# Sixteen of the 44 gate/up groups of a two-layer decoder trunk computed by Strassen's scheme, and most transposes of their results sent through DRAM

## The chip, the cores and the metric

One core of one Trainium2 chip runs the whole program. The metric is the device time of one execution in microseconds (us), the median of several runs of the same program. Engines are named as in the profile: PE is TensorE's matmul, PEld its weight load, DVE is VectorE, ACT is ScalarE, POOL is GpSimd, and SP is SyncE, which here only issues the loads of the weights.

## What is computed

Two decoder layers over 256 tokens of width 2048 in float32: a gated DeltaNet mixer, an FFN, an HGRN2 mixer, an FFN, each behind an RMS norm and with a residual add, and a final norm. The change touches the two FFNs alone:

```
D_MODEL, SEQ, DEPTH = 2048, 256, 2
D_FF = -(-8 * D_MODEL // (3 * 256)) * 256        # 5632

def rmsnorm(x, w, eps=EPS):
    xf = x.astype(jnp.float32)
    y = xf * lax.rsqrt(jnp.mean(xf * xf, axis=-1, keepdims=True) + eps)
    return (y * w.astype(jnp.float32)).astype(x.dtype)

def swiglu(h, w_gate, w_up, w_down):
    return (jax.nn.silu(h @ w_gate) * (h @ w_up)) @ w_down
...
    for layer in range(DEPTH):
        ...
        h = h + swiglu(rmsnorm(h, ffn_norm[layer]), ffn_w_gate[layer], ffn_w_up[layer], ffn_w_down[layer])
    return rmsnorm(h, final_norm)
```

## The kernel before

**Float32 products out of three.** Each operand is split into a part that the matmul's fast 32-bit type holds and the rest: `wh` and `wl` for a weight, `xt_h` and `xt_l` for the activations. A product is xh*wh + xh*wl + xl*wh, three matmuls into one PSUM accumulator. ACT makes `wh` (a rounding copy of `raw`), DVE makes `wl` (`raw` - `wh`).

**The stream.** All weights come in items of 128 x 1024 values (512 KB), in one order, through `stream`: SP loads `raw`, ACT and DVE split it, PE uses it. There are four `raw` buffers (RAW_BUFS) and four each of `wh` and `wl` (SPLIT_BUFS), so a split can be made while the items ahead of it are still being used. Items of one result make a `Group`: its matmuls collect in one PSUM tile `main` (two of these, of two banks each), and its `end` reads them out. Four more banks, `aux`, serve everything else.

**The FFN.** The 5632 hidden columns are cut into 22 gate/up groups of 256 gate and 256 up columns. A group is eight items; each item holds two k-tiles of 128 rows and 512 columns (gate beside up), and each k-tile is used for two halves of 128 tokens, three matmuls each: 96 matmuls of 512 columns a group, with a piece of the activations as the stationary side. `gate_up`'s `end` takes Silu of the gate on ACT (`sg`), multiplies by up on DVE (`h1`), and, for every second group, turns the pair's `h1` (token x 512) into `turned` (512 x token) by 16 DVE transposes of 32 partitions x 256 (`turn`), and splits that into `hth` and `htl`, the stationary side of the down product. The norm's factor `rstd`, one number per token, is applied at the read-out. `down` multiplies by the down weights, in four column groups of 512, adds the residual (`add_x`, with x kept in DRAM as `x_home`), and calls what follows. FF_PARTS = (12, 10): twelve gate/up groups, their share of the down product, then ten and theirs.

**Who sets the order.** The program is first recorded, then a planner (`plan`) gives each engine its fixed order: matmuls of the stream (`main`, and `aux` tiles marked `stream`) stay in the order in which they are recorded, everything else is placed by a table of costs and by how late it may be, on PE between the stream's matmuls. Engines run that order without changing it, and wait for one another through semaphores. `Recorder.issue` emits it, so almost all instructions have its line, L490.

In the names of the profile and of the order, `h` is `h1`, `main<-wh,xt_h` a matmul into `main` with `wh` moving and `xt_h` stationary, and buffer numbers stand after a `_`.

Of the kernel before, what the change touches and what calls it, by code (L numbers as in the profile page):

```python
# [17 lines left out]
P = 128  # L18
T = 256
# [5 lines left out]
FF_PARTS = (12, 10)  # L25
N_HGRN = 4
LEVELS = (64, 32, 16, 8, 4, 2, 1)
MASKED = LEVELS[2:]
AHEAD = 3
# [465 lines left out]
class Group:  # L495

    def __init__(self, chunks, mm, end, begin=None, apart=False, cols=False):
        self.chunks, self.mm, self.end, self.begin, self.apart = chunks, mm, end, begin, apart  # L500
        self.cols = cols
        self.halves = [
            c[:, at : at + 1024] for c in chunks for at in range(0, c.shape[1], 1024)
        ]


class Trunk:
# [22 lines left out]
    def apart(self):  # L530
        return self.aux(stream=True), self.aux(stream=True)

# [55 lines left out]
    def stream(self, groups):  # L588
        nc = self.nc
        flat = [(g, i) for g in groups for i in range(len(g.halves))]  # L590
        ready = {}

        def place(tag, g):
            w = self.tile(self.wsplit, [P, 1024], tag, F32R, ordered=True)
            v = nc.virtual(w)
            v.pad, v.cols = PAD, g.cols
            return w

        def load(n):
            g, i = flat[n]  # L600
            raw = self.tile(self.wraw, [P, 1024], "raw", ordered=True)
            nc.sync.dma_start(raw, g.halves[i])
# [3 lines left out]
            h = place("wh", g)  # L606
            nc.scalar.activation(h, raw, AF.Copy)
            low = place("wl", g)
            nc.vector.tensor_tensor(out=low, in0=raw, in1=h.bitcast(F32), op=ALU.subtract)
# [3 lines left out]
        for n, (g, i) in enumerate(flat):  # L613
            while loaded < min(n + AHEAD, len(flat)):
                load(loaded)
                loaded += 1
            if i == 0:
                if g.begin:
                    g.begin()
                g.ps = self.apart() if g.apart else self.main()  # L620
            g.mm(g.ps, i, *ready.pop(n))
            if i == len(g.halves) - 1:
                g.end(g.ps)
# [143 lines left out]
    def turn(self, out, x):  # L767

        out = out.rearrange("p n (t a s) -> p t n a s", t=2, s=32)
        x = x.rearrange("p t (n b s) -> p t n b s", n=4, s=32)  # L770
# [5 lines left out]

    def ffn(self, j, after):
        nc, a = self.nc, self.a
        hts, h1s = {}, {}

        def gate_up(gi):
            def end(ps):
                if gi % 2 == 0:
                    h1s[gi // 2] = self.tile(self.pool, [P, 2, 512], "h1", bufs=2)
                h1 = h1s[gi // 2]
# [976 lines left out]
```

## Time and profile before

| what | value |
|---|---|
| time, median of 3 runs (lowest to highest) | 2762.76 us (2762.22 to 2763.23) |
| the profiled execution: its time, its span | 2763.82 us, 2761.4 us |
| granted TensorE clock, mean | 0.999 |
| loads of gate/up weights, first and last issue | 806.2 us, 2623.3 us |
| loads of HGRN2 weights, first and last issue | 1529.8 us, 1913.0 us |
| turns of `h1` on DVE | 352 transposes, 153.5 us busy, 436 ns each |
| DVE's splits `wl` | 945, 1160.6 us busy, 1229 ns each |
| bytes moved | 580.52 MB, 210 GB/s |

The span is the time from the first to the last instruction of the profiled execution; its time lies 2.4 us above it. The first FFN lies between the last GDN products and the first HGRN2 load, the second runs from about 2036 us to the end. Busy time of an engine counts overlapping instructions once; on PE the ends of matmuls are modelled, so that the rate of a run of matmuls is read from their starts.

### The profile page before, as it was taken

To read this page: it belongs to the slowest core of one execution; us is meant where nothing else is said; L and a number is where in the kernel's file an instruction comes from. 1 tells how busy PE (TensorE), PEld (TensorE's weight loads), DVE (VectorE), ACT (ScalarE), POOL (GpSimd) and SP (SyncE) were. 2 spreads that over 40 slices of the span, in tenths; PEclk is the share of its full clock that TensorE was granted. 3 is DMA by queue.
4 is the path that set the end of the run, shared out by engine and by line. 5 is a ranking of instruction groups with operands and counts; after the bars stand their busy time and mean duration, and the time that the engine had idled before them with its cause. 6 is when DMAs were issued, how large, how long until landed. Compare 5 with 4: busy or idle time off the path is not lost.

```text
span 2761.4 us, 41091 instructions
## 1 busy us (share of the span) xinstructions
PE 2744.9 (99%) x15662; PEld 2328.7 (84%) x15662; DVE 1899.6 (69%) x2857; ACT 1428.3 (52%) x2010; POOL 251.4 (9%) x370
## 2 busy tenths in 40 slices
PE   9999999999999999999999999999999999999998
PEld 9888888888888888888888989988888888888887
DVE  7787888887766667546665687778657675456764
ACT  6646666565554444344444556556454444344443
POOL 1213222232110000000000100000100000000000
PEclk9999999999999999999999999999999999999999
DMA  7686668787786666766667655555776666766664
GB/s 260 201 281 222 190 211 284 210 276 219 225 256 203 195 193 193 225 224 194 193 192 219 221 166 179 172 166 178 236 257 192 193 194 209 224 209 193 193 201 160
DMA packets 162677, 580.52 MB, mean 210 GB/s; under 512 B 20138, under 2 KB 21306, under 8 KB 162352
## 3 DMA queue, kind: packets, MB, share of 16 engines
q1 hardware_dynamic: 138912, 503.15, 57.1%
q0 software_dynamic: 23280, 73.91, 8.5%
q8 instruction: 122, 2.00, 0.3%
q10 hardware_dynamic: 288, 0.85, 0.1%
q14 instruction: 75, 0.61, 0.1%
HBM read 550.52 MB, written 27.31 MB: 209 GB/s over the span
## 4 chain that ended last, share of the span: by engine, by line
PE 98%; ACT 0%; DVE 0%; issue 0%; DMA 0%; SPq 0%; POOLq 0%; POOL 0%; ACTq 0%
PE main L490 92%; PE aux L490 6%; DMA first<-in_x 0%; ACT dec L490 0%; DVE wl L490 0%; ACT wh L490 0%; DVE utmp L490 0%; SPq L490 0%; DVE pre L490 0%; ACT xt_h L490 0%; DVE u L490 0%; ACT y L490 0%; POOLq L1758 0%; ACT junk L490 0%; DVE xl L490 0%
## 5 line engine op out<-in xcount | busy, mean ns | idle before, releaser
L490 DVE TENSOR_TENSOR wl<-raw,wh 128x1024 fp32r<-128x1024 f32 x945 | 1160.6, 1229 | 754.3 <-ACT wh L490 742.6
L490 ACT ACTIVATE wh<-raw 128x1024 fp32r<-128x1024 f32 x945 | 1000.9, 1060 | 1221.8 <-PE main L490 1123.5
L490 PE MATMUL main<-wh,xt_h 128*128 128x512 f32 x2176 | 849.3, 390 | 0.8 <-ACT wh L490 0.8
L490 PE MATMUL main<-wl,xt_h 128*128 128x512 f32 x2176 | 848.5, 390 | 1.3 <-DVE wl L490 1.3
L490 PE MATMUL main<-wh,xt_l 128*128 128x512 f32 x2176 | 849.5, 390 | 0.0
L490 PEld LDWEIGHTS main<-wl,xt_h 128*128 128x128 f32 x2176 | 408.5, 188 | 85.6 <-DVE wl L490 1.6
L490 PEld LDWEIGHTS main<-wh,xt_h 128*128 128x128 f32 x2176 | 408.5, 188 | 85.1 <-ACT wh L490 1.2
L490 PEld LDWEIGHTS main<-wh,xt_l 128*128 128x128 f32 x2176 | 408.6, 188 | 84.5
L490 PE MATMUL main<-xt_h,wh 128*128 128x256 f32 (+1 forms) x1040 | 288.8, 278 | 0.7 <-ACT wh L490 0.7
L490 PE MATMUL main<-xt_h,wl 128*128 128x256 f32 (+1 forms) x1040 | 288.3, 277 | 0.9 <-DVE wl L490 0.9
L490 PE MATMUL main<-xt_l,wh 128*128 128x256 f32 (+1 forms) x1040 | 288.1, 277 | 0.3 <-DVE xt_l L490 0.3
L490 PE MATMUL main<-wh,htl 128*128 128x512 f32 x664 | 258.6, 389 | 0.0
L490 PE MATMUL main<-wl,hth 128*128 128x512 f32 x664 | 258.4, 389 | 0.0
L490 PE MATMUL main<-wh,hth 128*128 128x512 f32 x664 | 258.3, 389 | 0.0
L490 PEld LDWEIGHTS main<-xt_h,wh 128*128 128x128 f32 (+1 forms) x1040 | 194.5, 187 | 1.3 <-ACT wh L490 0.9
L490 PEld LDWEIGHTS main<-xt_h,wl 128*128 128x128 f32 (+1 forms) x1040 | 194.4, 187 | 1.2 <-DVE wl L490 1.1
L490 PEld LDWEIGHTS main<-xt_l,wh 128*128 128x128 f32 (+1 forms) x1040 | 194.4, 187 | 1.0 <-DVE xt_l L490 0.5
L490 DVE STREAM_TRANSPOSE turned<-h 32x256 f32<-32x256 f32 x352 | 153.5, 436 | 7.2
L490 PE MATMUL main<-wh,ot_l 128*128 128x512 f32 x384 | 151.3, 394 | 0.0
L490 PE MATMUL main<-wl,ot_h 128*128 128x512 f32 x384 | 150.5, 392 | 0.0
L490 PE MATMUL main<-wh,ot_h 128*128 128x512 f32 x384 | 150.5, 392 | 0.0
L490 PEld LDWEIGHTS main<-wl,hth 128*128 128x128 f32 x664 | 124.6, 188 | 25.9
(206 smaller groups left out, 2249.9 us busy)
## 6 DMA issues: line engine op xcount, KB each, us to landing
raw<-in_ffn_gu SPq DMA_DIRECT2D x352, 512.0 KB, 4.7
raw<-in_ffn_d SPq DMA_DIRECT2D x176, 512.0 KB, 4.8
raw<-in_hgrn_in SPq DMA_DIRECT2D x128, 512.0 KB, 4.0
raw<-in_gdn_kq SPq DMA_DIRECT2D x64, 512.0 KB, 5.6
raw<-in_gdn_v SPq DMA_DIRECT2D x64, 512.0 KB, 4.7
raw<-in_gdn_z SPq DMA_DIRECT2D x64, 512.0 KB, 4.8
raw<-in_gdn_out SPq DMA_DIRECT2D x64, 512.0 KB, 5.0
x_home<-x POOLq DMA_DIRECT2D x36, 512.0 KB, 6.3
```

Source lines behind the costliest of these rows:

```text
L490: getattr(getattr(tc.nc, op.eng), op.method)(*args, **kw)
```

## The change

**Mixed groups.** In eight of the 22 groups of each FFN (pairs 1, 4, 7 and 8) the 2x2 block product [A11 A12; A21 A22] x [B11 B12; B21 B22] is computed with seven block products. The blocks of A are the two halves of the tokens and the two halves of the 2048 rows; the blocks of B are those rows by gate and by up (256 columns). With s1 = A21 - A22, s2 = A11 - s1, s3 = A21 - A11, s4 = A12 - s2 and t1 = B11 + B12, t2 = B22 + B12, t3 = B22 + t1, t4 = t3 + B21, the products are P1 = A11 B11, P2 = A12 B21, P3 = s4 B22, P4 = A22 t4, P5 = s1 t1, P6 = s2 t3, P7 = s3 t2. Each is a half bank of 128 tokens x 256 columns, in four `aux` banks, over 8 k-tiles and three matmuls: 168 matmuls of 256 columns.

`mix_inputs` makes s1 to s4 once an FFN on DVE, from `xt_h` + `xt_l` times `rstd_row`, and splits them into `mixh` and `mixl` (for this, `rstd_row` is now made at each layer's start). For each of four steps `kk` of a mixed group two halves of the weights are loaded into a ring of four tiles `sraw`; DVE makes t1 to t4 in the other two, and all are split as before (of the first half only B11). The group's `end` combines the seven products, with `rstd` only on P1, P2 and P4.

**Order.** FF_PARTS becomes (8, 8, 6), and FF_PLAN writes out which mixed pair lies among which plain pairs or among the down items of the part before. `Group` gives way to single `Item`s, which `among` interleaves.

**Turns.** All pairs but 3, 6 and 10 (FF_QUICK) are turned through DRAM: four DVE transposes of 128 x 256 into `blocks`, one DMA to `blocks_home`, and four DMAs back into `turned`, on POOL's queue. The quick pairs are turned on DVE as before, but a group at a time, in 32 transposes of half the size.

```diff
-FF_PARTS = (12, 10)
+FF_PARTS = (8, 8, 6)
+FF_PLAN = (
+    "0 | 1:2,3",
+    "4:down | 7:5,6",
+    "8:down | 9 | 10",
+)
+FF_QUICK = (3, 6, 10)
...
+def among(few, many, tail):
+    out, done = [], 0
+    for i, item in enumerate(many):
+        out.append(item)
+        upto = min(len(few), -(-len(few) * (i + 1) // (len(many) - tail)))
+        out += few[done:upto]
+        done = upto
+    return out
...
-            raw = self.tile(self.wraw, [P, 1024], "raw", ordered=True)
-            nc.sync.dma_start(raw, g.halves[i])
+            raw = item.ring() if item.ring else self.tile(self.wraw, [P, 1024], "raw", ordered=True)
+            if item.src is not None:
+                nc.sync.dma_start(raw, item.src)
...
+            if item.pre:
+                item.pre(raw)
...
+    def turn_through(self, out, x):
...
+        for b in range(4):
+            self.nc.vector.transpose(
+                blocks[:, b, :].rearrange("p (n t s) -> p n t s", n=4, s=32), x[:, :, :, b, :]
+            )
+        self.nc.gpsimd.dma_start(home, blocks)
+        home = home.rearrange("(a f) b r -> b f a r", a=4)
+        for b in range(4):
+            self.nc.gpsimd.dma_start(out[32 * b : 32 * b + 32], home[b])
...
+            uses = {
+                1: (plain(0, 0), 0, 0), 2: (plain(2, 0), 0, 1), 3: (mixed(4), 1, 0), 7: (mixed(3), 1, 1),
+                5: (mixed(1), 2, 0), 6: (mixed(2), 2, 1), 4: (plain(2, 1), 3, 0),
+            }
...
+            def raw_ring():
+                return self.tile(self.pool, [P, 1024], "sraw", bufs=4, ordered=True)
...
+                def mm(wh, wl):
+                    for k in range(2):
+                        for n, cols in parts:
+                            sh, sl = uses[n][0](2 * kk + k)
+                            c = slice(cols(k), cols(k) + T)
+                            for m, (x, w) in enumerate(((sh, wh), (sh, wl), (sl, wh))):
+                                nc.tensor.matmul(
+                                    product(n), x, w[:, c],
...
+                items += [
+                    item(kk, halves[0], keep(0), [(1, lambda k: k * 512)], lambda x: quarters(x)[:, 0]),
+                    item(kk, halves[1], keep(1), [(2, lambda k: k * 512), (3, lambda k: k * 512 + T)]),
+                    item(kk, None, sums(0), [(5, lambda k: k * T), (7, lambda k: 512 + k * T)]),
+                    item(kk, None, sums(1), [(6, lambda k: k * T), (4, lambda k: 512 + k * T)]),
+                ]
...
+        items = self.gdn(self.next_input(1, True))
+        items += self.ffn(0, self.next_input(2, True))
+        items += self.hgrn(self.next_input(3, True))
```

**What moves, in three places.** PE in the first FFN, where the first mixed item begins. Before, the same stretch holds nothing but products of 512 columns:

```order
L490 MATMUL main_8903<-wh_8844,xt_l_16_72 128x512
L490 MATMUL main_8903<-wh_8864,xt_h_13_69 128x512
L490 MATMUL main_8903<-wl_8874,xt_h_13_69 128x512
L490 MATMUL main_8903<-wh_8864,xt_l_17_73 128x512
L490 MATMUL main_8903<-wh_8864,xt_h_13_69 128x512
```

and now, behind the last matmuls of a plain item (`wh_9210`), the products P1, P2 and P3 of the first step:

```order
L496 MATMUL main_9276<-wl_9246,xt_h_12_68 128x512
L496 MATMUL main_9276<-wh_9210,xt_l_16_72 128x512
L496 MATMUL aux_9300<-wh_9237,xt_h_12_68 128x256
L496 MATMUL aux_9300<-wl_9265,xt_h_12_68 128x256
L496 MATMUL aux_9300<-wh_9237,xt_l_16_72 128x256
```

One token half and 256 columns stand where two halves and 512 stood, and the accumulators are `aux` tiles.

DVE at the end of the first plain group. Before, it made one `wl` after another:

```order
L490 TENSOR_TENSOR wl_9089<-raw_9026,wh_9078 128x1024
L490 SCALAR_TENSOR_TENSOR h_1337_8885<-main_8903,rstd_59,sg_8886 128x256
L490 SCALAR_TENSOR_TENSOR h_1337_8885<-main_8903,rstd_59,sg_8887 128x256
L490 TENSOR_TENSOR wl_9110<-raw_9044,wh_9099 128x1024
L490 TENSOR_TENSOR wl_9128<-raw_9062,wh_9118 128x1024
```

and now:

```order
L496 TENSOR_TENSOR wl_9265<-sraw_8895,wh_9237 128x2x256
L496 TENSOR_TENSOR wl_9270<-sraw_8899,wh_9253 128x1024
L496 TENSOR_TENSOR sraw_9282<-sraw_8899,sraw_8900 128x512
L496 TENSOR_TENSOR mixl_8888<-h_1325_9234,mixh_8887 128x512
L496 TENSOR_TENSOR wl_9295<-raw_9177,wh_9278 128x1024
L496 TENSOR_TENSOR sraw_9282<-sraw_9282,sraw_8899 128x512
L496 SCALAR_TENSOR_TENSOR h_1348_9256<-main_9106,rstd_59,sg_9288 128x256
L496 TENSOR_TENSOR wl_9324<-sraw_8900,wh_9303 128x1024
L496 TENSOR_TENSOR wl_9337<-raw_9195,wh_9319 128x1024
L496 TENSOR_TENSOR wl_9345<-sraw_9282,wh_9334 128x1024
L496 TENSOR_TENSOR sraw_9359<-sraw_8901 128x512
```

Between two plain splits (`raw`) stand the sums into `sraw`, the splits of the mixed items and the last of `mix_inputs`; `sraw_8899` is read for the last time in the sixth of these rows, and its place is the next step's second half.

DVE at the turn of a pair. Before, the 16 transposes lay in runs of two to four between splits:

```order
L490 STREAM_TRANSPOSE turned_8888<-h_1337_8885 32x2x4x32 x3
L490 TENSOR_TENSOR wl_9283<-raw_9211,wh_9271 128x1024
L490 STREAM_TRANSPOSE turned_8888<-h_1337_8885 32x2x4x32 x4
L490 TENSOR_TENSOR wl_9307<-raw_9230,wh_9292 128x1024
L490 STREAM_TRANSPOSE turned_8888<-h_1337_8885 32x2x4x32 x3
```

and now, for the second half of pair 3:

```order
L496 TENSOR_TENSOR htl_8910<-turned_10490,hth_8909 128x512
L496 SCALAR_TENSOR_TENSOR h_1571_10301<-main_10290,rstd_59,sg_10536 128x256
L496 TENSOR_TENSOR sraw_10728<-sraw_10650 128x512
L496 TENSOR_TENSOR wl_10736<-raw_10597,wh_10716 128x1024
L496 TENSOR_TENSOR wl_10743<-sraw_10641,wh_10732 128x1024
L496 STREAM_TRANSPOSE turned_10490<-h_1571_10301 32x2x2x32 x16
L496 TENSOR_TENSOR wl_10807<-raw_10633,wh_10753 128x1024
```

The 16 transposes of that half now stand in one block ahead of the next `wl`.

More of the change, by code (lines that the diff above doesn't have):

```diff
@@ L813, in down @@
+        def down(part, cg, pairs):
             w = a[f"ffn_d{j}_{part}"]
+            lo = sum(FF_PARTS[:part]) // 2
             def operand(kt):
-                h, l = hts[first + kt // 4]
+                h, l = hts[pairs[kt // 4]]
                 return h[:, kt % 4, :], l[:, kt % 4, :]
```

331 lines of the change are left out of this document (244 added, 87 removed).

## The prediction

> **What bounds the kernel now.** I read the profile's first page, then the chain that ended last, then what TensorE waited for, then windows and timelines inside the feed-forward layers (FFN).
>
> ```profile
> PE 2744.9 (99%) x15662; PEld 2328.7 (84%) x15662; DVE 1899.6 (69%) x2857; ACT 1428.3 (52%) x2010; POOL 251.4 (9%) x370
> PE 98%; ACT 0%; DVE 0%; issue 0%; DMA 0%; SPq 0%; POOLq 0%; POOL 0%; ACTq 0%
> 828.78 636.50 PE main L490 x2808
> 2036.53 687.72 PE main L490 x3034
> PE main L490 <- DVE wl L490: 2.2, 2, 1.3
> ```
>
> The first row is busy time by engine, the second the chain by engine, the next two are the longest pieces of that chain (start, length), the last is PE's longest wait for another engine (total, times, longest). TensorE is busy from end to end; each FFN is one unbroken run of matmuls, and PE waited twice for a `wl` in the whole program. So the time falls by what is taken from PE, as long as VectorE (DVE) and ScalarE (ACT) keep the operands coming. In a plain FFN stretch they have room:
>
> ```profile
> 880.00:920.00 40.00, 40.00 (x179) 33.11 (x178) 25.88 (x33) 18.32 (x20) 0.00 (x0) 1.00 0.59 191
> 2639.97 1.06 ACT L490 ACTIVATE wh<-raw 128x1024 fp32r<-128x1024 f32 x1 [1.66 <-PE main L490]
> 2641.06 1.23 DVE L490 TENSOR_TENSOR wl<-raw,wh 128x1024 fp32r<-128x1024 f32 x1 [1.50 <-ACT wh L490]
> ```
>
> The window row has start:end, length, then busy time of PE, PEld, DVE, ACT, POOL, the granted clock (1.00) and the DMA share. ACT waits for PE to give back a `wh` buffer (four exist), DVE waits for ACT: both run as far ahead as the buffers let them.
>
> **PE's part: what 1/8 fewer columns are worth.** Two timelines of PE alone, first and last row of an even run:
>
> ```profile
> 1419.78 0.39 PE L490 MATMUL main<-wh,xt_h 128*128 128x512 f32 x1
> ...
> 1423.86 0.39 PE L490 MATMUL main<-wh,xt_h 128*128 128x512 f32 x1
> ```
> ```profile
> 39.79 0.28 PE L490 MATMUL main<-xt_h,wh 128*128 128x256 f32 x1
> ...
> 43.87 0.28 PE L490 MATMUL main<-xt_h,wh 128*128 128x256 f32 x1
> ```
> ```profile
> L490 PEld LDWEIGHTS main<-wh,xt_h 128*128 128x128 f32 x2176 | 408.5, 188 | 85.1 <-ACT wh L490 1.2
> L490 PEld LDWEIGHTS main<-xt_h,wh 128*128 128x128 f32 x1024 | 192.3, 188 | 1.3 <-ACT wh L490 0.9
> L490 PE MATMUL aux<-vjunk,ones x8: 270/274/275, 33.6 to 1557.4; 128*128 128x128 f32 x8
> ```
>
> In the first, 18 matmuls of 512 columns start in 4.08 us, 226.7 ns each; in the second 36 of 256 columns start in 4.08 us, 113.3 ns each, with one 128-column weight load per matmul in both (the first two rows of the third block: count, busy time, mean ns). Half the columns cost exactly half. A plain group has 16 k-tiles x 2 token halves x 3 = 96 matmuls of 512: 21.76 us. A mixed group has 7 products x 8 k-tiles x 3 = 168 of 256: 19.04 us. Saved: 2.72 us a group, 16 groups, **43.5 us**. In the measured 256-column case the weight was the stationary side and x moved; now x is stationary. Both load in the same 188 ns, and the 113 ns hid that load, so I take 113.3.
>
> The Trainium skill ("TensorE: Matmul & The Clock Gate", section "Wait — 56ns, not 53.3ns?") gives each matmul a fixed extra of about 2.5 ns. By that the 1152 additional matmuls would give back 2.9 us, an estimate from that page; the two runs above show no fixed part, so the trace speaks against it and it is not in the sum.
>
> PE also gets two rows of `rstd_row` more (two matmuls each, like the last row's 0.27 us): +1.2 us, rounded up.
>
> **DVE's part: does it still keep up?** This decides. DVE's busy time counts overlapping instructions; what matters in a full queue is start to start.
>
> ```profile
> 1704.43 0.69 DVE L490 TENSOR_TENSOR kp<-k,e 128x512 f32<-128x512 f32 x1
> 1705.04 0.68 DVE L490 TENSOR_TENSOR qp<-q,e 128x512 f32<-128x512 f32 x1
> 1705.64 1.22 DVE L490 TENSOR_TENSOR wl<-raw,wh 128x1024 fp32r<-128x1024 f32 x1
> 1706.78 1.28 DVE L490 TENSOR_TENSOR e<-b 128x512 f32<-128x512 f32 x2
> ...
> 1684.08 0.42 DVE L490 TENSOR_TENSOR e<-b 128x256 f32<-128x256 f32 x1
> 1684.42 0.29 DVE L490 COPY e<-b 128x256 f32<-128x256 f32 x1
> ...
> 2037.47 1.65 DVE L490 SCALAR_TENSOR_TENSOR xt_l<-aux,head,xt_h 128x256 fp32r<-128x256 f32 x4
> ...
> 2656.17 2.25 DVE L490 STREAM_TRANSPOSE turned<-h 32x256 f32<-32x256 f32 x5
> ```
>
> Steps: 0.60 us for 512 elements, 1.14 for 1024, 0.34 for 256, 0.39 for scalar_tensor_tensor of 256 ((1.65 - 0.48)/3), 0.45 for a transpose of 256. The quick turn's half-size transposes (128 elements) are not in the trace: between half and all of 0.45, I take 0.33.
>
> A mixed step (`kk`) splits one 512 and three 1024 tiles and adds four 512: 0.60 + 3 x 1.14 + 4 x 0.60 = 6.4 us; a mixed pair of groups has eight, 51.4, plus two ends of 0.39 + 6 x 0.34 + 0.60 = 3.0: 57.5 us. A turn through DRAM costs DVE 4 x 0.45 + 1.14 = 2.9 us (16 x 0.45 + 1.14 = 8.3 before); a quick pair 32 x 0.33 + 2 x 0.60 = 11.8. `mix_inputs` is 8 x 1.14 + 16 x 0.60 = 18.7 an FFN. By stretch of FF_PLAN, DVE against PE:
>
> - pairs 0, 1, 2, 3: 18.7 + six plain groups (48 x 1.14 + 12 x 0.39 = 59.4) + 57.5 + three turns 8.8 + 11.8 = 156 us; PE 6 x 21.76 + 2 x 19.04 = 169 us. 93%.
> - pairs 7, 5, 6: 39.6 + 57.5 + 5.9 + 11.8 = 115; PE 125. 92%.
> - each mixed pair beside a down part: 32 x 1.14 + 4 residual adds of 1.14 + 57.5 + 2.9 = 102; PE 125. 81%. The four residual adds that the third part brings to each FFN are in here.
>
> With the full durations in place of the steps (1.23, 0.68, 0.42) the first two come to 170 and 124, just PE's own time. Can DVE run that full? HGRN's windows answer:
>
> ```profile
> 1680.00:1720.00 40.00, 40.00 (x305) 34.82 (x305) 36.02 (x45) 26.65 (x32) 1.04 (x1) 1.00 0.59 184
> 1690.00:1700.00 10.00, 10.00 (x49) 8.41 (x49) 9.69 (x10) 6.14 (x8) 1.04 (x1) 1.00 0.58 186
> 1700.00:1710.00 10.00, 10.00 (x72) 8.13 (x71) 9.34 (x14) 6.60 (x8) 0.00 (x0) 1.00 0.61 184
> ```
>
> DVE 90% busy over 40 us and 95% over 20 us, PE never idle. So on average DVE keeps up. What remains is local. From the two rows at 2640, a `wl` is done 2.3 us after its `wh` could start, while three items are still ahead on PE: 3 x 2.72 - 2.3 = 5.9 us of lead between plain items, but 2.72 + 2 x 1.36 - 2.3 = 3.1 us with two mixed items (12 matmuls of 113 ns) among the three. The second halves of quick pairs 3 and 6 put 16 transposes in one block before the next `wl`: 5.3 us, 2.2 more than the lead. Four such places: **+8.8 us** (0 if the lead is whole there, up to 16 x 0.45 - 3.1 = 4.1 each). Pair 10's second half must be evacuated, turned and split within the four down items ahead of it (10.9 us) while DVE makes their `wl`: 5.3 + about 2 + 4 x 1.14 = 11.9: **+1 us**, twice.
>
> **ACT, DMA, POOL.** ACT splits the same tiles: 4 x (0.63 + 3 x 1.06), two copies and two Silus of 256, 17 us a mixed group, inside PE's 19 and the plain groups' slack (18.32 of 40 busy above). Bytes loaded stay; 16 turns of 512 KB add 8 MB each way.
>
> ```profile
> L490 ACT ACTIVATE wh<-raw 128x1024 fp32r<-128x1024 f32 x945 | 1000.9, 1060 | 1221.8 <-PE main L490 1123.5 <-ACT sg L490 16.8 <-ACT hth L490 15.2
> L490 ACT ACTIVATE junk<-x 128x512 f32<-128x512 f32 x34 | 21.5, 632 | 3.9 <-DVE x L490 3.4
> L490 ACT ACTIVATE sg<-main,rstd 128x256 f32<-128x256 f32 x88 | 36.3, 461 | 0.0
> raw<-in_ffn_gu SPq DMA_DIRECT2D x352, 512.0 KB, 4.7
> x_home<-x POOLq DMA_DIRECT2D x36, 512.0 KB, 6.3
> x<-x_home POOLq DMA_DIRECT2D x36, 512.0 KB, 5.7
> L490 DVE TENSOR_TENSOR wl<-raw,wh x44: 1218/1226/1226, 1120.6 to 1237.5; 128x1024 fp32r<-128x1024 f32 x44
> L490 DVE TENSOR_TENSOR wl<-raw,wh x105: 1199/1226/1943, 1639.0 to 1959.2; 128x1024 fp32r<-128x1024 f32 x105
> ```
>
> A `sraw` tile of step kk+1 can load only when DVE's sums of step kk have read the tile; behind that wait on SP stand the plain `raw` loads. By the new order about 6.5 us of DVE work lie between that release and the first use, a load lands in 4.7: hidden, with 1.8 to spare. A turn takes 3 (end) + 1.8 + 6.3 + 5.7 + POOL's issues of about 3 + split 2, some 22 us; pair 1's is wanted after six plain items and four down items with theirs between, about 32 us. POOL's queue holds the residual stores and loads behind it, wanted later still. All at nothing; if that cover went, a late pair would stop PE by the difference.
>
> The last two rows are DVE's `wl` (shortest/median/longest) while POOL only issued DMAs, and in HGRN, where POOL also copies and fills. The Trainium skill ("GPSIMD Engine Reference", Specifications) has POOL share its SBUF interface with DVE instructions of two SBUF inputs, which all added sums are. The second row fits (one of 1943 ns), but the first shows that issuing DMAs, all that POOL gains here, stretches nothing.
>
> **Sum.** Profiled execution 2763.8 (span 2761.4 and 2.4 around it) - 43.5 + 1.2 + 8.8 + 2 = 2732.3. That execution lies 1.1 above the median of the runs (2762.8), so **2731**.
>
> **Rivals.**
> - *All hidden*: the lead covers the blocks; 2763.8 - 42.3 - 1.1 = 2720. For it: the 20 us at 95% above. Against: shorter items, less lead.
> - *DVE paces the heavy stretches*: dependent sums don't overlap, so full durations count, at the 95% that HGRN showed: (170 + 124)/0.95 = 309 against PE's 294, 15.4 an FFN, 2751. For it: 93% leaves 23 us an FFN. Against: most neighbours in the new order are independent.
> - *DVE stands behind late inputs* (the other side): its queue is in order, and each wait for a `sraw` load, a product or ACT's `wh` holds all splits behind it. At full durations it decides from 294/(294 + 21) = 93% busy; at the 87% of a GDN slice (row below) it would be 338 against 294, +88, 2808: slower. Against: the HGRN rows.
> ```profile
> 320.00:360.00 40.00, 40.00 (x252) 32.73 (x252) 34.63 (x72) 21.84 (x34) 13.57 (x21) 1.00 0.79 241
> ```
> - *Turns land late*: 8 us at three places of each FFN, +48: 2768, about no change. Against: the 10 us of room.
> - *256 columns do not cost half* with x as the stationary side: from 129.5 ns a matmul (21.76/168) nothing is saved; with the load's own 188 ns unhidden it would be 31.6 us a group, 2921. Against: GDN's even 113.3.
>
> **How the numbers follow.** Chances: the forecast 0.45 (its own range 2724 to 2742), all hidden 0.25, DVE pacing 0.13, late inputs 0.08, late turns 0.06, dear matmuls 0.03. About 0.2% (5.5 us) can be told from no change. Faster: the first three and a third of the late turns, 0.85; same 0.04; slower 0.11. The range 2719 to 2754 takes the first three and leaves out 0.17.
>
> **What would show it.** PE: 128x256 matmuls `aux<-wh,...` at even 113 ns starts. PE's waits on DVE `wl` some 10 us in all, sitting at pairs 3 and 6; DVE some 90% busy from the start of each FFN for about 170 us. None on `htl` from a turn through DRAM, none on DMA. Wrong if PE's idle time exceeds 40 us, or if it is spread evenly over all mixed items (then DVE paces them), or if DVE's waits name `sraw` loads.

## The result: half of the forecast gain

| | before | changed |
|---|---|---|
| median of four runs each, us | 2762.99 | 2746.83 |
| range, us | 2762.22 to 2765.33 | 2745.67 to 2747.26 |
| changed / before | | 0.9939 (95%: 0.9922 to 0.9957) |
| profiled execution, us (span) | 2763.82 (2761.4) | 2747.26 (2745.6) |

The kernel became 16.2 us faster, where 31.8 were forecast. The time lies in the range, between the forecast and no change. From the page of the changed kernel, busy time by engine and the chain that ended last by engine:

```profile
PE 2727.6 (99%) x16822; PEld 2363.9 (86%) x16822; DVE 2169.4 (79%) x3309; ACT 1548.5 (56%) x2192; POOL 308.4 (11%) x466
PE 98%; ACT 0%; DVE 0%; issue 0%; DMA 0%; SPq 0%; POOLq 0%; POOL 0%; ACTq 0%
```

PE sets the end as before. It was idle for 2745.6 - 2727.6 = 18.0 us, before for 2761.4 - 2744.9 = 16.5. So idle time rose by 1.5 us, where 10.8 were forecast, and PE's busy time fell by 17.3 us, where 42.3 were forecast: no engine held PE up, and its own work became dearer than forecast. That is more than the whole of the 15.6 us that were expected and not seen. What PE waited for, the three longest sums and the row of the quick turns (total, times, longest):

```profile
PE main L496 <- DVE wl L496: 2.2, 2, 1.3
PE aux L496 <- DMA first<-in_x: 1.7, 2, 1.4
PE main L496 <- ACT wh L496: 1.5, 2, 0.8
...
PE main L496 <- ACT hth L496: 1.0, 4, 0.2
```

The first is the same row as before the change. There is no wait on a `wl` by a mixed item at all, none on a turn through DRAM and none on a `sraw` load; the quick turns show up as the last row, four waits on `hth` of 0.24 us. Two windows of the first FFN, the second around the quick turn of pair 3, in the columns of the prediction:

```profile
880.00:920.00 40.00, 40.00 (x231) 35.30 (x230) 34.63 (x44) 22.86 (x27) 2.79 (x5) 1.00 0.69 225
1000.00:1040.00 40.00, 39.74 (x226) 34.57 (x226) 37.74 (x56) 22.03 (x24) 2.90 (x5) 1.00 0.64 203
```

DVE is busy 34.63 and 37.74 of 40 us (25.88 in the first before), 87 and 94%, and PE keeps its 40.00 and 39.74. Now PE's own timeline in the changed kernel, one mixed item and what follows it (start, us):

```profile
903.07 0.28 PE L496 MATMUL aux<-wh,xt_h 128*128 128x256 f32 x1
903.18 0.28 PE L496 MATMUL aux<-wl,xt_h 128*128 128x256 f32 x1
903.30 0.28 PE L496 MATMUL aux<-wh,xt_l 128*128 128x256 f32 x1
...
904.38 0.28 PE L496 MATMUL aux<-wh,mixl 128*128 128x256 f32 x1
904.50 0.40 PE L496 MATMUL main<-wh,xt_h 128*128 128x512 f32 x1
904.73 0.40 PE L496 MATMUL main<-wl,xt_h 128*128 128x512 f32 x1
904.97 0.39 PE L496 MATMUL main<-wh,xt_l 128*128 128x512 f32 x1
...
905.66 0.39 PE L496 MATMUL main<-wh,xt_l 128*128 128x512 f32 x1
```

From 903.30 to 904.38 nine matmuls of 256 columns start in 1.08 us: 120.0 ns each, not 113.3. And after 904.50 five of 512 columns take 1.16 us, 232 ns each, before they return to 226.7. Over all 224 places where a mixed item is followed by plain ones, the five take 233, 236, 228, 233 and 231 ns (medians), together 27 ns above five times 226.7, while the first two of a mixed item take 7 ns less together than 2 x 120.

The starts of the whole trace, as means from one start to the next (gaps over 300 ns left out), in ns:

| | mixed, 256 columns | x stationary, 512 (gate/up and mixers) | down, 512 | projections with x moving, 256 |
|---|---|---|---|---|
| before | none | 226.90 | 226.71 | 114.65 |
| changed | 119.41 | 227.55 | 228.31 | 114.85 |

From these the account: 1,536 matmuls of 226.90 go (-348.5 us), 2,688 of 119.41 come (+321.0), a net -27.5 in place of -43.5. The 4,992 matmuls of 512 columns with x stationary that stay (2,688 of gate/up, the others in the two mixers, whose price did not move) are 0.65 ns dearer (+3.2), the 2,112 of the down projection 1.60 (+3.4). With 1.5 us more of idle time and 1.2 for the `rstd_row`s this is -18.2; the profiled executions differ by 16.6, which leaves 1.6 us. One window, in the changed kernel and before, shows a candidate (the column ahead of the last two is the granted clock):

```profile
8.00:12.00 4.00, 3.76 (x19) 3.76 (x20) 3.79 (x8) 3.22 (x9) 0.00 (x0) 0.57 0.98 355
```
```profile
8.00:12.00 4.00, 3.22 (x28) 3.22 (x29) 3.93 (x8) 3.63 (x11) 0.00 (x0) 1.00 0.98 355
```

Behind a wait of 1.42 us for the first inputs, the changed kernel's profiled execution has 3.4 us at a granted clock of 0.50, which is worth some 1.7 us.

So two questions go to the experiments: why does a matmul of 256 columns cost 120.0 ns here and 113.3 ns in the projections, and what do the changes of width cost? A third is whether DVE's headroom and the turns through DRAM were needed at all.

One thing differs between the two kinds of 256-column matmul beside the roles of x and the weight. The kernel pads its weight tiles so that in the groups with `cols` the stationary `wh` and `wl` lie at bytes 108 and 364 modulo 512 of a partition (`IN_COLS`); everything else that a large matmul reads, stationary or moving, plain or mixed, lies at byte 32 by the kernel's layout. That makes two theories: **placement** (the price hangs on where the operands lie) and **role** (a matmul with x stationary costs 6.7 ns more anywhere).

### The profile page after: what moved, and what is told of

Its sections match the earlier page's. It is cut to its first block, busy times and chain, and to the rows that moved or that the text cites. A ratio compares the mean times of both kernels' runs of the same rounds, so it can differ in the third digit from the quotient of the medians.

```text
span 2745.6 us, 44285 instructions
## 1 busy us (share of the span) xinstructions
PE 2727.6 (99%) x16822; PEld 2363.9 (86%) x16822; DVE 2169.4 (79%) x3309; ACT 1548.5 (56%) x2192; POOL 308.4 (11%) x466
## 4 chain that ended last, share of the span: by engine, by line
PE 98%; ACT 0%; DVE 0%; issue 0%; DMA 0%; SPq 0%; POOLq 0%; POOL 0%; ACTq 0%
PE main L496 81%; PE aux L496 18%; DMA first<-in_x 0%; ACT dec L496 0%; DVE wl L496 0%; ACT wh L496 0%; DVE utmp L496 0%; SPq L496 0%; DVE pre L496 0%; ACT xt_h L496 0%; DVE u L496 0%; ACT mixh L496 0%; POOLq L2007 0%; ACT junk L496 0%; DVE p L496 0%
## 5 line engine op out<-in xcount | busy, mean ns | idle before, releaser
L496 ACT ACTIVATE wh<-raw 128x1024 fp32r<-128x1024 f32 x817 | 864.4, 1059 | 937.9 <-PE main L496 803.2
L496 DVE TENSOR_TENSOR wl<-raw,wh 128x1024 fp32r<-128x1024 f32 x817 | 1003.1, 1229 | 426.4 <-ACT wh L496 416.8
L496 PE MATMUL main<-wh,xt_h 128*128 128x512 f32 x1664 | 651.8, 392 | 0.8 <-ACT wh L496 0.8
L496 PE MATMUL main<-wl,xt_h 128*128 128x512 f32 x1664 | 651.0, 391 | 1.3 <-DVE wl L496 1.3
L496 PE MATMUL main<-wh,xt_l 128*128 128x512 f32 x1664 | 650.6, 391 | 0.0
L496 PEld LDWEIGHTS main<-wh,xt_l 128*128 128x128 f32 x1664 | 312.6, 188 | 65.2
L496 PEld LDWEIGHTS main<-wh,xt_h 128*128 128x128 f32 x1664 | 312.9, 188 | 62.8 <-ACT wh L496 1.2
L496 ACT ACTIVATE wh<-sraw 128x1024 fp32r<-128x1024 f32 (+1 forms) x256 | 243.4, 951 | 141.6 <-PE main L496 98.1
L496 DVE TENSOR_TENSOR wl<-sraw,wh 128x1024 fp32r<-128x1024 f32 (+1 forms) x256 | 278.4, 1088 | 28.2 <-ACT wh L496 26.8
L496 PEld LDWEIGHTS main<-wh,htl 128*128 128x128 f32 x680 | 127.7, 188 | 29.1 <-DVE htl L496 1.7
```

The source lines that it names most:

```text
L496: getattr(getattr(tc.nc, op.eng), op.method)(*args, **kw)
```

## Experiments

Times are medians, and the ratio is to the kernel before on the same chip, with its 95% interval. Prices are means from start to start, as in the table above.

**The projections' weights at byte 32.**

```diff
-            v.pad, v.cols = PAD, cols
+            v.pad, v.cols = PAD, False
```

> The changed kernel with one thing altered: the projections that run the other way round (weight tile stationary, x moving, 256 columns) keep their weights in SBUF at the byte offset that the rows groups use (32 modulo 512) instead of 108 and 364. In the changed kernel these 3,072 matmuls start every 113.3 ns, while the 2,688 of the mixed groups (x stationary, 256 columns too) start every 120.0 ns. Theory 'placement' (the price of a matmul beside its columns hangs on where its two operands lie in SBUF): the 113.3 ns become 120.0, 3,072 x 6.7 ns = 20.5 us more, about 2,767 us. Theory 'role' (a matmul with x stationary and the weight moving costs 6.7 ns more wherever its operands lie): they stay at 113.3 ns and the time stays near 2,747 us.

Measured: 2766.02 us, ratio 1.0008 (0.9998 to 1.0017); against the changed kernel's ratio that is 0.69% or 19 us more. An even run of the projections in the changed kernel, and the same in this one:

```profile
39.10 0.28 PE L496 MATMUL main<-xt_h,wh 128*128 128x256 f32 x1
...
44.54 0.28 PE L496 MATMUL main<-xt_h,wh 128*128 128x256 f32 x1
```
```profile
39.07 0.28 PE L496 MATMUL main<-xt_l,wh 128*128 128x256 f32 x1
...
44.83 0.28 PE L496 MATMUL main<-xt_l,wh 128*128 128x256 f32 x1
```

48 starts in 5.44 us are 113.3 ns; 48 starts in 5.76 us are 120.0. The same instructions on the same data, 76 and 332 bytes further down: the mean went from 114.85 to 120.80 ns, and with it the whole gain of the change was lost again. Placement holds, role falls for this half of the question.

**The mixed groups' moving weights at 108 and 364.**

```diff
-                return Item(src, mm, pre, ring=raw_ring, part=part)
+                return Item(src, mm, pre, cols=True, ring=raw_ring, part=part)
```

> The changed kernel with the mixed groups' moving weights at byte offsets 108 and 364 modulo 512 instead of 32; their stationary operands (xt and the mixed inputs) stay at 32. Placement, if it is the distance between the two operands that counts: the 2,688 matmuls go from 120.0 to 113.3 ns, 17.9 us less, about 2,729 us. Placement, if it is the stationary operand's own address that counts: no change, 2,747 us. Role: no change, 2,747 us.

Measured: 2738.50 us, ratio 0.9907 (0.9892 to 0.9922), 8.3 us below the changed kernel. The mixed price is 117.13 ns: between the two expectations. That is 2,688 x 2.3 = 6.1 us; most of the rest came from the plain matmuls behind the mixed items (three slow ones instead of five; down 228.31 to 227.87, x stationary 227.55 to 227.38). One group by form, in the changed kernel and here (busy us, mean ns):

```profile
L496 PE MATMUL aux<-wl,mixh 128*128 128x256 f32 x512 | 144.9, 283 | 0.0
```
```profile
L496 PE MATMUL aux<-wl,mixh 128*128 128x256 f32 x512 | 143.1, 280 | 0.0
```

The distance alone is not the rule, since the same distance the other way round gave only a third of the 6.7 ns; but x is stationary here and the price fell, so role falls in the mixed groups too.

**The mixed inputs at 108 and 364.**

```diff
-        both = [self.tile(self.pool, [P, 4096], f"mix{x}", F32R) for x in "hl"]
+        both = [self.tile(self.pool, [P, 4224], f"mix{x}", F32R)[:, at : at + 4096] for x, at in (("h", 19), ("l", 83))]
```

> The changed kernel with the mixed inputs (mixh, mixl), which are the stationary operand in four of a mixed group's seven products, at byte offsets 108 and 364 modulo 512; the other three products keep xt at 32, and the moving weights stay at 32. Placement by either reading (distance, or the stationary operand's own address): the four products' 1,536 matmuls of 256 columns go from 120.0 to 113.3 ns, 10.2 us less, about 2,737 us, and the other three stay at 120.0. Role: nothing changes, 2,747 us.

Measured: 2740.70 us, ratio 0.9915 (0.9900 to 0.9929), 6.1 us below the changed kernel. Within mixed items the matmuls with `mixh` and `mixl` come to 113 to 118 ns (means 115.9 for `wh,mixh` and 114.5 for `wh,mixl`), those with `xt_h` ahead of another `xt` stay at 119 to 120. The moved products move and the others do not, by six tenths of what was expected: where `xt` at 32 and `mix` at 108 alternate, the price lies between.

**Strassen alone undone.** The mixed pairs are plain groups again, each in one piece instead of spread among the others, and the mixed inputs are not formed. This kernel does 1/7 more of multiplication in these groups than the changed one.

```diff
-                items += among(mixed_pair(int(mix)), many, 2 if beside == "down" else 6)
+                few = gate_up(2 * int(mix)) + gate_up(2 * int(mix) + 1)
+                at = 0 if beside == "down" else 16
+                items += many[:at] + few + many[at:]
...
-            self.mix_inputs()
```

> The changed kernel with Strassen's products alone undone: the sixteen mixed groups are plain groups of 512 columns again at the same place beside the down projection, and the mixed inputs are not formed. Three parts, the turns through DRAM and the row of rstd stay. If the 512-column matmul keeps its 226.8 ns and the whole new order costs PE nothing, PE's saving is gone and the kernel takes as long as before the change, 2,763 to 2,765 us. If the new order (turns through DRAM, three parts, weights fetched two ways) costs something of its own that Strassen's saving pays for, it takes more than 2,768 us.

Measured: 2764.78 us, ratio 1.0004 (0.9995 to 1.0014). From its page:

```profile
PE 2747.1 (99%) x15670; PEld 2329.2 (84%) x15670; DVE 1837.2 (66%) x2781; ACT 1429.1 (52%) x2016; POOL 307.4 (11%) x466
```

With x stationary 226.91, down 226.71 ns: the plain matmuls have their price of before again, so the slower ones belong to the mixed items. The new order costs PE some 2 us (2747.1 against 2744.9, the two `rstd_row`s in it) and gives DVE 62 us back (1837.2 against 1899.6) through the turns. Strassen's products are worth 2764.8 - 2746.8 = 18 us to the time and cost DVE 2169.4 - 1837.2 = 332 us.

**All of x at 108 and 364.** As in the run with the mixed inputs moved, and:

```diff
-IN_COLS = {"wh": 108, "wl": 364}
+IN_COLS = {"wh": 184, "wl": 440}
...
-        self.xt_h = [t([P, 4, T], f"xt_h{i}", F32R) for i in range(4)]
-        self.xt_l = [t([P, 4, T], f"xt_l{i}", F32R) for i in range(4)]
+        self.xt_h, self.xt_l = four("xt_h", 19, 24), four("xt_l", 59, 104)
```

> The changed kernel with every stationary operand of the mixed groups moved: xt_h and mixh at byte offset 108 modulo 512, xt_l and mixl at 364, the moving weights left at 32 (and, for the projections in which x is the moving operand, the weights moved on by the same 76 bytes, so that the distance stays). The run in which mixh and mixl alone were moved took 2,740.7 us and brought their four products from 120.0 to about 115.9 ns on average. Placement: now all seven products come down by as much, 2,688 x 4 ns, about 11 us below the changed kernel in all, about 2,736 us. If the 512-column matmuls with xt stationary (4,992 of them at 226.7 ns) hang on the placement in the same way, they fall by up to 6.7 ns each, another 33 us, about 2,703 us, while those with ht or ot stationary stay at 226.7 ns. Role: 2,747 us, nothing changes. If the projections with x moving lose their 113.3 ns because x has moved, up to 20 us are added.

Measured: 2776.60 us, ratio 1.0045 (1.0030 to 1.0060), 30 us above the changed kernel, though its mixed price is the lowest of all: 115.21 ns, with 113 or 114 for most. The 512-column matmuls with `xt` stationary went up, from 227.55 to 233.23 ns (+28 us), and the projections, from 114.85 to 119.09 (+13 us), though `xt_h` and the weights had kept their distance (`xt_l`, at 364, had not); those on `ht` and `ot`, which were not moved, kept 228.35 and 227.42. The hoped-for 33 us had the wrong sign: the placement that suits 256 columns costs 512 columns 5.7 ns each. It also shows that not the distance alone decides.

**Mixed items in whole steps of four.**

```diff
-        upto = min(len(few), -(-len(few) * (i + 1) // (len(many) - tail)))
+        upto = min(len(few), -(-len(few) * (i + 1) // (len(many) - tail)) // 4 * 4)
```

> The changed kernel with the mixed group's items put among the plain ones in whole steps of four, so that PE changes between 256 and 512 columns fewer times (now 224 times each way). In the changed kernel the five 512-column matmuls after each mixed item take 29 ns more than 5 x 226.7 together, and the first mixed matmul 6.7 ns less than its 120.0. Theory 'each change of width costs': with about a quarter to a third of the changes left, some 3 to 4 us less, about 2,743 us, with the plain matmuls near 227 ns on average. Theory 'the slower 512s come of something else that the mixed groups bring (their DVE or DMA work on SBUF)': they stay near 228.5 ns on average wherever the items stand, 2,747 us. If the order also starves PE (DVE's four input sums of a step fall closer together), waits of PE on DVE wl show up and the time goes over 2,749 us.

Measured: 2772.55 us (2764.08 to 2778.94), ratio 1.0029 (1.0018 to 1.0041). Both parts of the expectation came true, and the bad one is the larger. There are 64 changes of width each way instead of 224; after each stand the same 233, 236, 228, 233, 231 ns, and the plain means fall from 227.55 to 227.15 and from 228.31 to 227.22, together 4.3 us less. But PE now waits:

```profile
PE aux L496 <- DVE wl L496: 13.7, 12, 3.1
PE main L496 <- ACT hth L496: 6.7, 4, 1.7
```

Twelve waits on `wl` by mixed items: four mixed items in a row (42 matmuls of 120 ns) last 5.0 us on PE and bring DVE 6.4 us of work. PE's busy time rose too, by 9.9 us: in the profiled execution six of the waits in the FFNs, of 1.7 to 3.1 us, are followed by 3.4 us at a granted clock of 0.50. The ten times scatter with the clock, from a mean of 0.998 in the two shortest to 0.994 or 0.995 in the two longest. The price of a change of width is real, and spreading the items is worth more than it.

**All pairs turned on DVE.**

```diff
-FF_QUICK = (3, 6, 10)
+FF_QUICK = tuple(range(11))
```

The mixed pairs call `turned_half` too.

> The changed kernel with all eleven pairs of an FFN turned on DVE, as before the change, instead of eight of them through DRAM; the mixed groups keep their products. This takes the DRAM turns away (16 of 22 in the two FFNs) and gives DVE 32 small transposes for 4 large ones in each of those pairs. If DVE's headroom in the stretches with mixed groups (90 to 95% busy in the changed kernel) is what the turns through DRAM were needed for, DVE passes 100% there, PE waits on DVE wl and on banks, and the time goes up by 10 to 40 us, 2,757 to 2,787 us. If DVE can make it up between the mixed groups, the time stays within 3 us of 2,747 and the turns through DRAM were not needed for time.

Measured: 2818.90 us, ratio 1.0198 (1.0181 to 1.0215), 72 us above the changed kernel and more than expected. PE's largest wait by sum, then a window of 10 us and the 3 us in it that are slowest (the column ahead of the last two is the granted clock), then PE's timeline behind one of the longest waits:

```profile
PE main L496 <- ACT hth L496: 36.9, 14, 4.4
```
```profile
1020.00:1030.00 10.00, 5.56 (x20) 4.04 (x19) 9.57 (x27) 2.63 (x3) 0.00 (x0) 0.67 0.32 105
...
1027.00:1030.00 3.00, 3.00 (x7) 2.41 (x8) 2.88 (x7) 0.73 (x1) 0.00 (x0) 0.50 0.00 0
```
```profile
1025.62 0.79 PE L496 MATMUL main<-wh,hth 128*128 128x512 f32 x1 [4.35 <-ACT hth L496]
...
1027.52 0.63 PE L496 MATMUL main<-wh,hth 128*128 128x512 f32 x1
...
1029.66 0.63 PE L496 MATMUL main<-wh,htl 128*128 128x512 f32 x1
...
1030.66 0.39 PE L496 MATMUL main<-wh,htl 128*128 128x512 f32 x1
```

DVE is full (9.57 of 10 us) and PE stands in front of the down projection, because the last pairs' turns come late; `wl` itself is hardly waited for. The second cost is in the clock: it fell to 0.50 at 1023.5, 2.2 us into the wait of 4.35 us, and stays there until 1030.3; five starts in 2.14 us make 427 ns (the median at eight such places) for 512 columns. Mixed matmuls of 256 columns at that clock start every 213 to 214 ns. Of the 72 us, 44.9 are more idle time and 26.8 more busy time on PE. So the turns through DRAM are what lets DVE carry Strassen's sums.

**Prices by placement, group by group.** Two single executions in which each mixed group, and sixteen plain ones, have their own placement; first with all stationary operands at 32:

```diff
-            want = IN_COLS[v.tag] if v.cols else 32 + n % 2 * 512
+            want = (IN_COLS if v.cols is True else v.cols)[v.tag] if v.cols else 32 + n % 2 * 512
...
-                return Item(src, mm, pre, ring=raw_ring, part=part)
+                return Item(src, mm, pre, cols=shifted(SHIFTS[8 * j + (2, 3, 8, 9, 14, 15, 16, 17).index(gi)]), ring=raw_ring, part=part)
```

> The disputed price measured by itself: the changed kernel with another placement of the moving weights for each of the sixteen mixed groups, and for sixteen of the twenty-eight plain ones (wh at byte 32 + s and wl at 288 + s modulo 512, s from 0 to 240 in sixteen steps); all stationary operands stay at 32, and the other plain groups and the down projections stay as they are for control. What is read is the time from start to start of each group's matmuls, not the whole time. Placement: the 256-column matmuls spread between 113 and 120 ns by group, and some placement gives 113; the 512-column ones, at 226.7 now, spread too, between about 220 and 235 ns. Role: 120.0 ns and 226.7 ns whatever the placement. Whole time: somewhere between 2,735 and 2,770 us, by the sum of these.

then with the mixed inputs at 108 and 364:

> The same reading of prices by group as in the run before (wh at byte 32 + s and wl at 288 + s, another s for each of the sixteen mixed groups), now with the mixed inputs, the stationary operand of four of the seven products, at 108 and 364 modulo 512 instead of 32. With all stationary operands at 32 the groups took 116.0 (s = 28) to 119.3 ns (s = 0, 108, 172) per matmul of 256 columns. If the price hangs on the two operands together, the products with mixh and mixl change with s in another way than those with xt, and at s = 0 (the placement in which the projections with x moving take 113.3 ns) those in a run of mixed stationaries come to 113 to 114 ns. If it hangs on the moving weights alone, both kinds of product show the prices of the run before again, 116.0 at s = 28 and 119 at s = 0.

Measured (2744.55 and 2746.00 us in one execution each), mean prices in ns by the shift s (plain ones from the ninth of a run on, so that no change of width is in them, and gaps over 300 ns left out):

| s | 0 | 12 | 28 | 44 | 64 | 76 | 92 | 108 | 128 | 140 | 160 | 172 | 192 | 204 | 224 | 240 |
|---|---|---|---|---|---|---|---|---|---|---|---|---|---|---|---|---|
| mixed, all at 32 | 118.9 | 117.1 | 116.0 | 117.8 | 117.8 | 117.2 | 118.8 | 119.3 | 118.4 | 117.2 | 118.9 | 119.3 | 116.6 | 117.7 | 118.3 | 117.3 |
| plain 512, all at 32 | 226.8 | 229.0 | 227.0 | 230.3 | 229.0 | 228.6 | 232.4 | 226.7 | 232.4 | 231.1 | 234.8 | 230.7 | 232.5 | 231.2 | 233.0 | 236.3 |
| `xt` products, mix at 108 | 118.3 | 117.6 | 115.9 | 117.9 | 118.0 | 117.5 | 118.8 | 118.2 | 118.1 | 117.3 | 118.6 | 118.8 | 117.5 | 118.0 | 118.4 | 118.6 |
| `mix` products, mix at 108 | 116.3 | 117.0 | 118.1 | 117.5 | 116.9 | 119.4 | 116.3 | 117.6 | 118.9 | 117.1 | 118.5 | 119.3 | 118.5 | 117.7 | 121.1 | 117.1 |

The mixed price spreads over 116.0 to 119.3 ns and the plain one over 226.7 to 236.3; the plain groups' present 226.7 is the lowest, which none of these shifts undercuts. 113 was not reached by moving the weights alone. In the second run the `xt` products follow the first run's row to within some 1 ns while the `mix` products, whose stationary side was moved, do not: at s = 28 they rise from 116.0 to 118.1, at s = 0 they fall from 119.2 to 116.3. Within runs of mixed stationaries the price at s = 0 is 115.0 on average with a median of 114, a little above the 113 to 114 expected. The price hangs on the two operands together.

**Mixed items two at a time.** The edit is the one of the whole steps, with `// 2 * 2`.

> The changed kernel with the mixed items put among the plain ones two at a time: PE changes between 256 and 512 columns 128 times each way instead of 224 (in whole steps of four it was 64, with the same 233, 236, 228, 233, 231 ns after each, but PE waited 14 us on DVE wl and 9 on hth and htl, and the time went up to 2,772). If each change costs 22 ns net (29 after it, 6.7 saved ahead of it), 96 fewer give 2.1 us: 2,744 to 2,745 us, provided that DVE keeps ahead. If two items at a time already starve PE, waits on DVE wl and on ACT hth show up and the time goes over 2,750 us.

Measured: 2754.25 us, ratio 0.9964 (0.9950 to 0.9978), 7.4 us above the changed kernel. Its waits on a mixed item's `wl` are gone, the one on `hth` is the 6.7 us of the run before, and one window holds a visible part of it:

```profile
PE main L496 <- ACT hth L496: 6.7, 4, 1.7
```
```profile
1020.00:1030.00 10.00, 8.51 (x50) 7.35 (x48) 9.69 (x22) 5.34 (x7) 0.00 (x0) 1.00 0.39 127
```

These waits cost more than their length. PE's timeline behind the second of the four, and the stretch of half clock in it:

```profile
1287.74 0.50 PE L496 MATMUL main<-wh,hth 128*128 128x512 f32 x1 [1.67 <-ACT hth L496]
...
1289.00 0.63 PE L496 MATMUL main<-wh,hth 128*128 128x512 f32 x1
...
1291.56 0.59 PE L496 MATMUL main<-wh,hth 128*128 128x512 f32 x1
```
```profile
1288.56:1291.97 3.41, 3.41 (x8) 2.66 (x9) 3.41 (x5) 0.00 (x0) 0.00 (x0) 0.50 0.70 228
```

Three of the four waits of 1.67 us are followed by such a stretch: six starts in 2.56 us, 427 ns each. At half speed 3.4 us lose 1.7, together 5.1 us, and with 6.5 us more of idle time than in the changed kernel and about 2 us saved by fewer changes of width that accounts for the 9.5 us between the two profiled executions.

**The cheapest placement of the first reading, for all mixed groups.** The edit of the readings, with `cols={"wh": 60, "wl": 316}` (s = 28).

> The changed kernel with one thing altered: the moving weights of all mixed groups at bytes 60 (wh) and 316 (wl) modulo 512, the placement that was cheapest in the first reading by groups (116.04 ns for each matmul of 256 columns there, against 119.41 ns on average in the changed kernel). Placement: 2,688 x 3.4 ns = 9.1 us less than the changed kernel, about 2,738 us. If the 116 ns of that one group came of its neighbours and not of its placement, the mean stays above 117.5 ns and the time above 2,741 us. Role: 2,747 us.

**And the same with two items at a time, rounded up.**

```diff
-        upto = min(len(few), -(-len(few) * (i + 1) // (len(many) - tail)))
+        upto = min(len(few), -(-len(few) * (i + 1) // (len(many) - tail) // 2) * 2)
```

> The kernel of the run beside it (weights at 60 and 316), and the mixed items put among the plain ones two at a time with the count rounded up instead of down, so that the mixed pair ends no later than in the changed kernel (128 changes of width each way instead of 224). The run that rounded down took 7.4 us more than the changed kernel; its PE waited 6.7 us on ACT hth and ran short of work around 1,020 to 1,040 us. Theory 'that loss was the later end of the mixed pair': here the wait on hth is 1 us again and the saved changes show, 96 x 22 ns = 2.1 us below the run beside it, about 2,736 us. Theory 'it was DVE's work coming in double portions': the waits on hth, or on wl, are there again and the time is 5 to 8 us above the run beside it, 2,743 to 2,746 us.

Measured: 2741.34 us, ratio 0.9918 (0.9902 to 0.9935), and 2740.56 us, ratio 0.9916 (0.9901 to 0.9931). The first got its mixed price (116.01 ns, 9.1 us less) but not its time: behind each mixed item eight matmuls of 512 are slow instead of five, and the down price rose from 228.31 to 228.93 ns, and that with x stationary from 227.55 to 227.8, so 5.5 us were left. The second is the same within the runs' spread. It saved changes of width (down 227.95 ns), and its wait on `hth` is half of the rounded-down run's:

```profile
PE main L496 <- ACT hth L496: 3.3, 2, 1.7
```

Rounding up took away half of that wait, not all, so the later end of the mixed pair explains half of it; the doubled portions of DVE's work are the likely rest, which no run isolates.

Best of all kernels run is the one with the moving weights at 108 and 364: 2738.5 us, one argument changed, against 2746.8 of the changed kernel and 2763.5 of the kernel before on its chip.

## Why the prediction held in sign and missed in size

**"What bounds the kernel now"** held: PE to the end, 98% of the chain before and after.

**"Half the columns cost exactly half", 43.5 us: here it failed.** The step compared 226.7 with 113.3 ns and found no fixed part. But the two numbers come from two placements. The clock can be read from this study: at half the granted clock 512 columns took 427 ns and 256 columns 213 to 214 (the run with all pairs on DVE), in proportion, so at full clock 512 columns are 213.5 ns and 256 are 106.8, if nothing stands beside them at half the clock. What stands beside the columns is then 13.2 ns in the plain groups and 6.5 in the projections: not proportional, but two different fixed parts of which one happens to be half the other, like the columns. With the plain groups' placement a 256-column matmul has their 13.2 and costs 120.0. That took 2,688 x (119.4 - 113.3) = 16.4 us from the 43.5. The prediction had written the condition down ("now x is stationary") and named the case as a rival at 0.03, "256 columns do not cost half"; its reason, the role, was shown wrong, and 129.5 ns, the price at which it saw no gain at all, was not reached. The kernel's own planner prices a matmul in `op.cost` at 0.0133 us plus its columns over 2400, 120.0 ns for 256, which the prediction did not use.

The Trainium skill ("TensorE: Matmul & The Clock Gate", section "Wait — 56ns, not 53.3ns?") has a fixed part of 2.5 ns per matmul, only at the full clock. That there is one, and none at the half clock, the traces here bear out (427 ns for 512 columns, 213 to 214 for 256); its size is 6.5 or 13.2 ns here. Weighing it and leaving it out was the same mistake as the term itself. Another sentence of that page (section "Step-by-step: what each phase is for") has the next weights load without taking read bandwidth from the running matmul, through two read ports. The run with the projections' weights at 32 shows that this is not the whole of it: the same stream cost 113.3 or 120.0 ns by the weights' addresses alone. Whether the two reads meet, or something else makes the difference, no run shows.

**A cost that the prediction did not have**: the change of width. Each of 224 changes back to 512 columns makes the next five matmuls 27 ns slower together (29 in two of the expectations), 6.1 of the 6.6 us by which the plain matmuls rose. Undoing Strassen brought 226.9 ns back, and fewer changes brought it nearly back; why five, and why three or eight with other placements, stays open.

**"+1.2" for `rstd_row`** is within the 2.2 us of PE time by which the run without Strassen's products exceeds the kernel before.

**"+8.8" at the quick pairs and "+1 twice": not there.** The block was sized rightly; the lead was not. DVE at pair 3, and PE's first matmul behind it, in the changed kernel:

```profile
1021.71 5.04 DVE L496 STREAM_TRANSPOSE turned<-h 32x128 f32<-32x128 f32 x16
1026.78 1.23 DVE L496 TENSOR_TENSOR wl<-raw,wh 128x1024 fp32r<-128x1024 f32 x1
```
```profile
1027.90 0.50 PE L496 MATMUL main<-wh,hth 128*128 128x512 f32 x1 [0.24 <-ACT hth L496]
```

The block and the step to the next `wl` took 5.07 us (5.3 forecast). When it began, PE had two mixed items and a plain one ahead of it, 1.44 + 2.74 + 1.44 = 5.6 us and not 3.1: the 2.3 us that the prediction subtracted from them had been spent before. The waits sit where they were forecast, at the second halves of pairs 3 and 6 of both FFNs, but what came late is the turned half itself and not the next `wl`: four waits of 0.24 us on `hth` in place of four of 2.2 on `wl`. That the lead is what counts is right: where items came in fours, the same DVE work cost 13.7 us of waits.

**"On average DVE keeps up"**, the turns and the loads: all held (DVE busy 150.5 of the 170 us from 828 on, no wait of PE on a turn through DRAM, `sraw` landing in 5.1 us). The two misses were of opposite sign, 10.8 us of stalls of which 1.5 came against 23 of dearer matmuls (16.4 and 6.6), so the sum landed nearer than its largest term. That is luck: with the stalls that were forecast and the matmul prices that were measured the time would have been about 2756 us, above the range.

**The rivals.** "All hidden" was right on DVE and had the same 43.5. "DVE paces the heavy stretches" gives a time near the one measured, 2751, by a mechanism that did not take place: PE was busy through those stretches. Late inputs and late turns did not occur in this order, but the all-on-DVE run is a case of late turns before the down projection, at +72 us.

## What to carry to other kernels

A price per matmul taken from another place of the kernel carries that place's operand addresses with it: read start to start at the full and the half clock, separate the columns from the rest, and compare the byte offsets of both operands before scaling. When two widths share one PE queue, count the changes between them as a cost, but don't pay for fewer changes with the lead of the engine that feeds the queue. A wait of PE that is not hidden can cost about twice its length, by the clock behind it: read the granted clock after each one. A trial that gives every group its own placement reads sixteen prices in one execution; the price behind the group must be read too, as the run at 60 and 316 shows.

## What was unexpected of the hardware

- The start-to-start time of a matmul depends on the SBUF byte offsets of its stationary and moving operand together: 113.3 to 121.1 ns for 256 columns, 226.7 to 236.3 for 512, with the best placement of the one costing the other (233.2 against 227.6 ns). The rule behind it was not found; neither the distance nor one operand's address alone explains the readings.
- After a change from 256 to 512 columns the next matmuls of 512 columns are slower, five of them by 27 ns together (three with the moving weights at 108, eight at 60).
- A PE wait cost more than itself: in a wait of 4.35 us the granted clock fell to 0.50 and stayed there for 6.8 us, and matmuls of 512 columns took 427 ns; three of four waits of 1.67 us were followed by 3.4 us at 0.50. The Trainium skill ("TensorE: Matmul & The Clock Gate", section "Part 1: The HAM clock gate (the "warmup" mystery)") halves the clock after an idle window of about 3.4 us; in these traces shorter waits were enough.
